# The gate of the layer's last stage as 2 by 2 block products with seven products

## The chip, the cores and the metric

One core of one Trainium2 chip runs the kernel; float32 data, batch 1, 512 tokens. The metric is the device time of one execution in microseconds (us). Before the change it is 706.38 us, the median of three runs (705.05 to 706.64).

## The reference, cut to what matters

One layer: three groups of attention heads with one input and one output projection, a gated MLP with a width-3 convolution, and a last stage that adds a gated per-layer embedding. The change is in the last stage, and in how the weights of the MLP's down projection are made ready.

```python
h = h + concat([o_a, o_b, o_c]) @ w_out[i]
h = h + conv_gated_mlp(rms_norm(h, ln_ffn[i]), w_up[i], conv_w[i], conv_b[i], w_down[i])
gate = sigmoid(rms_norm(h, ln_ple[i]) @ w_ple_gate[i])      # 512 x 1024 by 1024 x 1024
h = h + (p[i] @ w_ple_proj[i]) * gate
```

## The kernel before, in words

Activations lie transposed, features on the 128 partitions and the 512 tokens along the row. A float32 matrix product is made as three products of rounded parts (`mm3`): each operand is split into a high part, which ScalarE writes with a cast (rows `w_hi`, `Th`, `g_ah`, `xh`), and a low part, operand minus high part (rows `w_lo`, `Tl`, `g_al`, `xl`), and TensorE adds high by high, high by low and low by high. `split` (line 208) and `split_of` (line 1084) do this for weights: a load on SP's queue into one of 6 raw tiles, a cast on ScalarE, a subtraction on VectorE, and one of 7 pairs of high and low tiles that is free again when its last matmul has run.

**The stages.** Attention and the output projection, to about 290 us; a short stage that normalises; the up projection (tiles `u`), with the first parts of the down projection (tiles `dn_X`, `dn_Y`, `dn_Z`) among it, to 606 us; the rest of the down projection, to 653.9 us; the gate (tiles `pg`), to the end.

**Seven products.** The down projection works in 2 by 2 blocks: rows of weights in two halves (pairs of 128-row blocks), columns in two halves, tokens in two halves of `H` = 256. Seven products of block sums take the place of eight (`PRODUCTS`, `Down`, line 1338). The sums on the weights' side (`S1`, `S2`, `1e2e`, `1oS2`) are made in DRAM: copies on SP's queue during attention (`COPIES`, `copy_sum`), then 40 adding transfers on GpSimd's queue (`add_sums`, line 1185), one at a time: a semaphore holds each until the one before has landed. The sums on the activations' side are made by `left` (line 1206): four VectorE operations into tile `sm`, three casts and three low parts, 7 blocks of 256 columns for a pair of feature blocks. Each finished product is added to `h` by VectorE out of PSUM (`add_h`).

**The gate before.** `split3` casts and splits the finished `h` blocks into `Th` and `Tl`. `gate` takes 8 output blocks of 128 rows, 8 blocks of depth each, three matmuls of 512 columns; the last output block is done in two halves of 256. Weights come as 16 tiles of 512 columns (`row_weights`) with the gain `ln_ple` multiplied in while they are split. The norm's factor comes from squares of `h` (ScalarE), their sum (GpSimd, the last two on VectorE) and one matmul `pst`; it is multiplied onto each finished block, then the sigmoid, the product with the embedding (`ppl`, loaded on GpSimd's queue) and the addition of `h` follow.

**The order.** From the up projection on, every engine's order is made when the program is built: tasks with durations are placed by a planner (the loop at the end of the kernel) that knows engine times, ring slots and due times worked back from TensorE's order. It writes each engine's queue; on the chip each engine runs its queue in order.

Of the kernel before, what the change touches and what calls it, by code (L numbers as in the profile page):

```python
# [15 lines left out]
P = 128  # L16
# [50 lines left out]
_sums = sorted([(f, "u", f) for f in SEVEN] + [(PHASES[ph + 1] + 3, "d", ph) for ph in range(len(PHASES) - 1)])  # L67
# [11 lines left out]
def kernel(ctx: ExitStack, tc: tile.TileContext, x, xt0, xt, pt_in, small, bias_c,  # L79
                             w_in, w_out, w_up, w_usum, w_down, w_dsum, w_dadd, w_ple_gate, w_ple_proj, out):  # L80
# [68 lines left out]
    ROOM, NARROW = 128, 16  # L149
# [58 lines left out]
    def split(t, n, gain=None, to=None, eng=dve, c0=0, lead=None):  # L208

        if lead is not None:  # L210
            whole = [in_turn(q, NHI) for q in ("hi", "lo")]
            a, b = lead * P, (lead + 1) * P
            for i, j, c in ((0, a, c0), (a, b, 2 * c0), (b, n, 5 * c0)):
                if i < j:
                    hi, lo = (q[:, i + c : j + c] for q in whole)
                    act.copy(hi, t[:, i:j])
                    eng.tensor_tensor(out=lo, in0=t[:, i:j], in1=f32(hi), op=ALU.subtract)
            return whole
        hi, lo = to or [in_turn(q, NHI)[:, c0 : c0 + n] for q in ("hi", "lo")]
        if gain is None:  # L220
            act.copy(hi, t[:, :n])
            eng.tensor_tensor(out=lo, in0=t[:, :n], in1=f32(hi), op=ALU.subtract)
# [819 lines left out]
    COUNT = {"raw": NRAW, "hi": NHI, "conv": CONV, "pin": 1, "left": 3, "x": 3, "z": 2, "s": 2, "t": 3, "o": 1}  # L1042
# [17 lines left out]
    def tile_of(n, name, src=None, tag="raw", deps=()):  # L1060
# [4 lines left out]
        def do():  # L1065
            w.t = raw_tile() if tag == "raw" else mtmp(F32, 1, name)
            if src is not None:
                sp.dma_start(out=w.t[:, :n], in_=src)

        w.load = Task("load" if tag == "raw" else "side load", [("dma", n * 0.00139 if src is not None else 0)], do, deps, [w.raw])  # L1070
        return w

    class Group:


        def __init__(self, name):
            self.slot, self.tiles, self.name = Slot("left"), None, name

        def get(self, i, n):
            if self.tiles is None:  # L1080
                self.tiles = [q.rearrange("p j c -> p (j c)") for q in left_tiles(self.name)]
            return [q[:, i * S : i * S + n] for q in self.tiles]

    def split_of(w, deps=(), gain=None, group=None, i=0, c0=0):

        w.c0, w.lead = c0, None
        w.hi_slot = Slot("hi") if group is None else group.slot
        makes = [w.hi_slot] if not w.hi_slot.users else []

        def do():  # L1090
            w.hi, w.lo = split(w.t, w.n, gain, None if group is None else group.get(i, w.n), c0=c0, lead=w.lead)

        w.split = Task("do", [AC(w.n), DV(w.n * (1 if gain is None else 1.12))], do, (w.load, *deps), makes, [w.raw] + ([] if makes else [w.hi_slot]))
# [6 lines left out]
    def part(w, j, n=P):  # L1100
        c = j * n
        if w.lead is not None:
            c += w.c0 * (1 if j < w.lead else 2 if j == w.lead else 5)
# [28 lines left out]
    def down_weights(ph, n, name, tag="raw"):  # L1132
# [4 lines left out]
        return lambda what: split_of(tile_of(m, f"{name}_{what}", src[what], tag, SUM_TASKS.get(("d", ph), ()) if "S" in what or "2e" in what else ()), c0=NARROW)  # L1137

    def row_weights(src, name, gain=None, group=None, i=0):
        return split_of(tile_of(S, name, src), LAST_X if isinstance(group, Rest) else (), gain, group, i)  # L1140

# [43 lines left out]
    def add_sums(f):  # L1185
# [4 lines left out]
        def do(to, src):  # L1190
# [3 lines left out]
            if state:  # L1194
                tc.add_manual_dep(ins, state["last"].name, mybir.DependencyInfo(
                    mybir.DependencyClass.Sync, mybir.DependencyReason.DATA), reason="one adding transfer at a time")
            state["last"] = ins

        last = b
        for _, *key in _sums:  # L1200
            key = tuple(key)
            for to, src in add_parts(key):
                last = Task("add", [("pool", 1.2), ("acc", 3.2 if key[0] == "u" else 4.2)], lambda to=to, src=src: do(to, src), [last], (), [slot] if last is b else ())
                SUM_TASKS.setdefault(key, []).append(last)

    def left(f):

        tt = dve.tensor_tensor
        v = {}

        place, sums = Slot("left" if f < 18 else "x"), Slot("pin")

        def one():
            v["r"] = r1, r2 = G[f], G[f + 1]
            if f < 18:
                v["hl"] = left_tiles(f"g{f}")
            else:
                v["hl"] = tuple(q.rearrange("p a b c -> p (a b) c")[:, (f - 18) // 2 * 7 :][:, :7] for q in (Xh, Xl))
            hi, lo = v["hl"]
            v["sm"] = sm = mp.tile([P, 4, H], F32, tag="pin", bufs=1, name=f"sm_{f}")  # L1220
            tt(out=sm[:, 0], in0=r1[:, H:], in1=r1[:, :H], op=ALU.subtract)
            tt(out=sm[:, 2], in0=r2[:, :H], in1=r1[:, :H], op=ALU.subtract)
            act.copy(hi[:, 0], r1[:, H:])
            act.copy(hi[:, 1:3], r2.rearrange("p (j c) -> p j c", j=2))

        def two():
# [3 lines left out]
            act.copy(hi[:, 3:], sm)  # L1230
# [10 lines left out]

        (d1, s1), (d2, s2) = done_f[f], done_f[f + 1]
        a = Task("do", [DV(H), DV(H), AC(H), AC(S)], one, (d1, d2, LAST_X[0] if f >= 18 else None), [place, sums], [s1, s2])
        a = Task("do", [DV(H), DV(H), AC(2 * S)], two, [a], (), [s1, s2, place, sums])
        b = Task("do", [DV(H), DV(S)], three, [a], (), [s1, s2, place])
        c = Task("do", [DV(2 * S)], four, [a], (), [place, sums])
        CHAIN[f] = (b, c), place

# [296 lines left out]
    SPLIT3 = {}  # L1545

    def split3(n, b, c):

        g, ks, ts = n, slice(2 * c, 2 * c + 2), slice(b * H, (b + 1) * H)
        dh, dl = (T[g][:, ks, ts] for T in (Th, Tl))  # L1550

        def do():
            act.copy(dh, hblk(b, n, c))
            dve.tensor_tensor(out=dl, in0=hblk(b, n, c), in1=f32(dh), op=ALU.subtract)

        SPLIT3[n, b, c] = Task("do", [AC(S), DV(S)], do, [H_ADDS[n, q] for q, p in PRODUCTS.items() if p[3:5] == (b, c)] + ALL_UP)

    ALL_UP = [q for q in TASKS if q.kind == "pe"][-1:]
    sq_slots, sum_slot = [], Slot("pin")
    v3 = {}  # L1560

    def square3(j):

        s = Slot("conv")
        sq_slots.append(s)
        first = j == 0

        def do():
            if first:
                pin = mp.tile([P, D + 88], F32, tag="pin", bufs=1, name="sums3")  # L1570
                v3["sums"], v3["rb"] = pin[:, :S], pin[:, S:D]
            v3[j] = v3["sums"] if first else mtmp(F32, 1, f"n3_sq{j}")
            act.activation(v3[j], hj(j), AF.Square)
# [3 lines left out]

        deps = [H_ADDS[j // 4, q] for q, p in PRODUCTS.items() if p[4] == j // 2 % 2]
        if first:
            v3["last"] = Task("do", [AC(S)], do, deps, [sum_slot])  # L1580
        else:
            a = Task("do", [AC(S)], do, deps, [s])
# [5 lines left out]
    for b in range(2):  # L1588
        for c in range(2):
            split3(0, b, c)  # L1590
# [5 lines left out]
    for c in range(2):  # L1596
        for b in range(2):
            split3(1, b, c)
    for j in range(KD):
        square3(j)  # L1600
    pst_slot, root_slots = Slot("t"), [Slot("conv"), Slot("conv")]

    def sums3():
        v3["pst"] = total("t", v3["sums"])

    def roots3():
        roots(v3["pst"], v3["rb"], mtmp(F32, 1, "mt"), mtmp(F32, 1, "rsq"))

    def gate(j, c0, c1, at_k={}):
# [193 lines left out]
```

## Time and profile before

| what | value |
|---|---|
| median of three runs | 706.38 us |
| the profiled execution, as timed | 706.92 us |
| its span in the profile | 705.1 us |
| TensorE busy | 688.7 us (98%) |
| VectorE, ScalarE, GpSimd busy | 547.9, 395.5, 223.1 us |
| granted clock, mean | 0.997 |
| moved by DMA | 116.5 MB |

Times in the profile are us from the span's start. PE is TensorE, DVE VectorE, ACT ScalarE, POOL GpSimd, SPq the queue of SyncE that issues transfers. L105 is the line of a helper through which nearly all operations go, so rows are told apart by the names of tiles. A row of the timeline gives the start, the duration, and in brackets the idle time before it with what ended it. Durations of neighbouring rows overlap: an operation's issue is read from the difference of two starts.

### The profile page before, as it was taken

How to read it: one execution, taken by the hardware profiler on the slowest of the kernel's cores; microseconds unless marked ns; L12 is line 12 of the kernel's file. 1: busy time of each engine (PE TensorE's matmuls, PEld its weight loads, DVE VectorE, ACT ScalarE, POOL GpSimd, SP SyncE). 2: the span in 40 equal slices, each digit the busy share in tenths (PEclk: the TensorE clock that was granted, in tenths of full speed). 3: DMA queues.
4: the chain of work that ended last, by engine and by line, in shares of the span. 5: the costliest groups of instructions: out<-in, count | busy, mean ns of one | idle time of the engine just before them, and what ended most of it. 6: DMA issues, size and time to landing. Idle time of an engine off the chain costs nothing.

```text
span 705.1 us, 11575 instructions
## 1 busy us (share of the span) xinstructions
PE 688.7 (98%) x4028; PEld 616.2 (87%) x4028; DVE 547.9 (78%) x1123; ACT 395.5 (56%) x750; POOL 223.1 (32%) x324
## 2 busy tenths in 40 slices
PE   9999999999999999999999999999999999999997
PEld 8988888988999988868888899988988888999786
DVE  7668887888878875788878875798786787889764
ACT  6646766766656753565545653465444554646731
POOL 4676676767665440420110110110101110001310
PEclk9999999999999999999999999999999999999999
DMA  9453668746335213353686788787997675652531
GB/s 329 179 150 94 197 183 240 201 170 189 102 134 192 95 69 120 124 167 127 180 175 126 209 217 186 178 190 186 251 208 153 138 205 108 210 188 91 170 108 71
DMA packets 48471, 116.52 MB, mean 165 GB/s; under 512 B 5494, under 2 KB 7158, under 8 KB 48412
## 3 DMA queue, kind: packets, MB, share of 16 engines
q1 hardware_dynamic: 40476, 96.59, 42.3%
q0 software_dynamic: 7648, 18.88, 16.8%
q8 instruction: 32, 0.52, 0.3%
q10 hardware_dynamic: 288, 0.30, 0.1%
q14 instruction: 27, 0.22, 0.1%
HBM read 108.53 MB, written 31.47 MB: 199 GB/s over the span
## 4 chain that ended last, share of the span: by engine, by line
PE 78%; DVE 7%; DMA 6%; ACT 4%; POOL 2%; issue 2%; SPq 0%; DVEq 0%; ACTq 0%; POOLq 0%
PE u L105 30%; PE dn_X L105 8%; PE C_z L105 6%; PE pg L105 6%; PE wo L105 5%; PE dn_Y L105 4%; PE B_z L105 4%; PE dn_Z L105 2%; DMA bias_B<-fk_d 1%; DMA h<-in_x_dram 1%; PE sX L105 1%; PE A_z L105 1%; DMA waq<-in_w_in_dram 1%; PE C_s L105 1%; PE C_po L105 1%
## 5 line engine op out<-in xcount | busy, mean ns | idle before, releaser
L105 PE MATMUL u<-Tl,w_hi 128*128 128x512 f32 x320 | 125.0, 390 | 0.5 <-DVE Tl L105 0.5
L105 PE MATMUL u<-Th,w_hi 128*128 128x512 f32 x320 | 124.8, 390 | 0.0
L105 PE MATMUL u<-Th,w_lo 128*128 128x512 f32 x320 | 124.7, 390 | 0.0
L105 ACT CAST w_hi<-w_raw 128x768 fp32r<-128x768 f32 (+4 forms) x129 | 90.0, 724 | 58.0 <-PE u L105 17.7
L105 DVE TENSOR_TENSOR w_lo<-w_raw,w_hi 128x768 fp32r<-128x768 f32 (+3 forms) x127 | 102.7, 832 | 15.3 <-ACT w_hi L105 14.6
L105 DVE SCALAR_TENSOR_TENSOR c<-u,cols,c 128x511 f32<-128x511 f32 x80 | 59.7, 747 | 23.3 <-ACT c L105 22.3
L105 PEld LDWEIGHTS u<-Tl,w_hi 128*128 128x128 f32 x320 | 60.1, 188 | 13.4 <-DVE Tl L105 1.3
L105 PEld LDWEIGHTS u<-Th,w_lo 128*128 128x128 f32 x320 | 60.1, 188 | 12.6 <-POOL w_lo L105 0.2
L105 PEld LDWEIGHTS u<-Th,w_hi 128*128 128x128 f32 x320 | 60.1, 188 | 12.6 <-ACT Th L105 0.5
L105 ACT ACTIVATE c<-u,cols 128x512 f32<-128x512 f32 x40 | 31.1, 777 | 26.3 <-PE u L105 26.1
L105 POOL DMA_DIRECT2D dsum<-in_w_dadd_dram x16 | 13.1, 821 | 90.2 <-DMA dsum<-in_w_dadd_dram 64.8
L105 POOL DMA_DIRECT2D dsum<-dsum x16 | 13.0, 811 | 87.3 <-DMA dsum<-dsum 58.0
L105 PE MATMUL dn_X<-g_ah,w_hi 128*128 128x256 f32 x144 | 39.8, 277 | 0.0
L105 PE MATMUL dn_X<-g_ah,w_lo 128*128 128x256 f32 x144 | 39.8, 277 | 0.0
L105 PE MATMUL dn_X<-g_al,w_hi 128*128 128x256 f32 x144 | 39.8, 276 | 0.0
L105 PE MATMUL B_z<-B_h,Th 128*128 128x384 f32 x96 | 34.4, 358 | 0.8 <-DVE B_zn L105 0.6
L105 PE MATMUL C_z<-C_h,Th 128*128 128x384 f32 x96 | 34.2, 357 | 0.0
L105 PE MATMUL B_z<-B_h,Tl 128*128 128x384 f32 x96 | 32.4, 337 | 0.0
L105 PE MATMUL C_z<-C_h,Tl 128*128 128x384 f32 x96 | 32.3, 337 | 0.0
L105 PE MATMUL C_z<-C_l,Th 128*128 128x384 f32 x96 | 32.2, 336 | 0.0
L105 PE MATMUL B_z<-B_l,Th 128*128 128x384 f32 x96 | 32.2, 336 | 0.0
L105 PEld LDWEIGHTS dn_X<-g_al,w_hi 128*128 128x128 f32 x144 | 27.1, 188 | 0.3
(506 smaller groups left out, 2076.9 us busy)
## 6 DMA issues: line engine op xcount, KB each, us to landing
w_raw<-in_w_up_dram SPq DMA_DIRECT2D x44, 384.0 KB, 4.9
dsum<-in_w_dsum_dram SPq DMA_DIRECT2D x12, 768.0 KB, 6.8
w_raw<-dsum SPq DMA_DIRECT2D x24, 384.0 KB, 4.0
w_raw<-in_w_down_dram SPq DMA_DIRECT2D x18, 384.0 KB, 4.8
w_raw<-in_w_up_dram SPq DMA_DIRECT2D x20, 256.0 KB, 4.9
B_r<-in_w_in_dram SPq DMA_DIRECT2D x12, 384.0 KB, 3.7
C_r<-in_w_in_dram SPq DMA_DIRECT2D x12, 384.0 KB, 4.4
dsum<-in_w_dadd_dram POOLq DMA_DIRECT2D x12, 384.0 KB, 6.7
```

What stands on the lines that cost most here:

```text
L105: ins = getattr(self.eng, op)(*a, **k)
```

## The change

The gate is computed like the down projection. `h` times the gain goes through `left_blocks` (the body of `left`, now shared) for four pairs of feature blocks (`gate_left`): pairs 0 and 1 into the tiles `Th`/`Tl`, pairs 2 and 3 into the `g_ah`/`g_al` ring. Seven products for each of two halves of the output take three matmuls of 256 columns per pair and half; accumulators lie in the tags of `TAGS`. Weights come as tiles of 768 columns for pairs 0 to 2 and of three times 256 for pair 3, from `w_down4` (the gate's weights in the blocks' layout) or from sums in DRAM: 4 more copies (1 MB each) in the attention stage, and 8 more adding transfers of 512 KB. Adding transfers now wait for the one before the last, so two are under way. The products start with pairs 0 and 1 of the three that need no other result, in both halves; then pair 2, the norm's matmul, and pair 3.

Work that moves to GpSimd: the low parts of all 14 weight tiles of the down projection's last phase (`dn_...`, 512 columns), of 9 of the gate's 19 weight tiles (`BY_POOL`), four of the eight squares, and the two closing operations of three output blocks. GpSimd no longer issues the loads of `ppl`; SP does. In the planner, a task without VectorE work is now placed first if it can start before the next VectorE task.

The core of the diff:

```diff
-_sums = sorted([(f, "u", f) for f in SEVEN] + [(PHASES[ph + 1] + 3, "d", ph) for ph in range(len(PHASES) - 1)])
+_sums = sorted([(f, "u", f) for f in SEVEN] + [(PHASES[ph + 1] + 3, "d", ph) for ph in range(len(PHASES) - 1)]) + [(NF, "d", len(PHASES) - 1)]
+GATE = len(PHASES) - 1
...
-        return lambda what: split_of(tile_of(m, f"{name}_{what}", src[what], tag, SUM_TASKS.get(("d", ph), ()) if "S" in what or "2e" in what else ()), c0=NARROW)
+        return lambda what: split_of(tile_of(m, f"{name}_{what}", src[what], tag, SUM_TASKS.get(("d", ph), ()) if "S" in what or "2e" in what else ()), NARROW, pool if ph == 3 else None)
...
             ins = pool.dma_start(out=to, in_=src, accum_op=ALU.add, max_dma_last_dim=6144).ins
-            if state:
-                tc.add_manual_dep(ins, state["last"].name, mybir.DependencyInfo(
+            state["all"] = [*state.get("all", ()), ins]
+            if len(state["all"]) > 2:
+                tc.add_manual_dep(ins, state["all"][-3].name, mybir.DependencyInfo(
...
+            if j < 4:
+                pool.tensor_tensor(out=v3[j], in0=hj(j), in1=hj(j), op=ALU.mult)
+            else:
+                act.activation(v3[j], hj(j), AF.Square)
...
+    def gate_left(p):
+                act.activation(v[i], hj(2 * p + i), AF.Copy, scale=col(C_PLE, 2 * p + i))
...
+        left_blocks(("h", p), lambda: (v[0], v[1]), in_t if p < 2 else lambda: left_tiles(f"h{p}"), Slot("T" if p < 2 else "left"),
+                    hs + (ALL_UP if p < 2 else []), used, True)
...
+    def gate_product(n, what, pairs, w, b0, halves=(0, 1), begin=False, stop=False):
...
+            for i, p in enumerate(pairs):
+                hi, lo = LEFT["h", p]
+                for t in halves:
+                    q = accs[n, an][t % len(tags)]
+                    mm3(q[:, t * H : (t + 1) * H], *part(w, b0 + 2 * i + t), hi[:, li], lo[:, li],
+                        begin and i == 0 and t < len(tags), stop and i == len(pairs) - 1, skip_group_check=True)
...
+        e = pool if (n, what) in ((1, "1o"), (0, "1oS2"), (1, "1e2e")) else dve
...
+                e.tensor_tensor(out=y, in0=y, in1=pp, op=ALU.mult)
+                e.tensor_tensor(out=y, in0=y, in1=hblk(b, n, c)[:, t0:t1], op=ALU.add)
...
+    BY_POOL = {2, 4, 6, 8, 10, 12, 14, 16, 18}
...
+            main = [x for x, q in tr if any(e == "dve" for e, _ in q.parts)]
+            first_at = max(min(main, default=1e9), clock["dve"])
+            side = [(x, q) for x, q in tr if x < first_at and all(e != "dve" for e, _ in q.parts)]
+            if side:
+                tr, first_at = side, min(x for x, _ in side)
```

Three places show what the change makes of the engines' queues. First GpSimd's queue behind the last adding transfers, before the change (`sums` and `n_sq` belong to the norm; `ppl` are loads of the embedding):

```order
L105 DMA dsum_3484<-in_w_dadd_dram 128x512 x4
L105 DMA dsum_3484<-dsum_3484 128x512 x4
L105 TENSOR_TENSOR sums_7101<-sums_7101,n_sq_7103 128x512
L105 TENSOR_TENSOR sums_7101<-sums_7101,n_sq_7116 128x512
L105 TENSOR_TENSOR sums_7101<-sums_7101,n_sq_7184 128x512
L105 TENSOR_TENSOR sums_7101<-sums_7101,n_sq_7187 128x512
L105 TENSOR_TENSOR sums_7101<-sums_7101,n_sq_7189 128x512
L105 DMA ppl_0_7234<-pp_d 128x512
```

With the change ten low parts of `dn_...` tiles (weights of the down projection's last phase) stand directly behind the last adding transfer; then follow these rows, up to the first low part of a gate weight (`w_raw` of 128x768; `sums<-h` and `n_sq<-h` are squares):

```order
L106 TENSOR_TENSOR sums_4097<-h 128x512
L106 TENSOR_TENSOR n_sq_6977<-h 128x512
L106 TENSOR_TENSOR w_lo_3983<-dn_1_1o,w_hi_3982 128x512
L106 TENSOR_TENSOR sums_4097<-sums_4097,n_sq_6977 128x512
L106 TENSOR_TENSOR w_lo_4044<-dn_1_1e2e,w_hi_4043 128x512
L106 TENSOR_TENSOR n_sq_7064<-h 128x512
L106 TENSOR_TENSOR w_lo_3935<-dn_1_1oS_6777,w_hi_3934 128x512
L106 TENSOR_TENSOR n_sq_7135<-h 128x512
L106 TENSOR_TENSOR w_lo_3967<-dn_1_2o,w_hi_3966 128x512
L106 TENSOR_TENSOR sums_4097<-sums_4097,n_sq_7064 128x512
L106 TENSOR_TENSOR sums_4097<-sums_4097,n_sq_7135 128x512
L106 TENSOR_TENSOR w_lo_3990<-w_raw_3867,w_hi_3989 128x768
```

Where five additions and the issue of nine loads stood, 38 operations with two inputs in SBUF stand now (30 of 512 columns, 8 of 768), all of them behind the last adding transfer.

Second, VectorE in the down projection's last stretch, where the first half's sums into `h` end, before the change (`h<-h,dn_...` is an addition out of PSUM):

```order
L105 TENSOR_TENSOR h<-h,dn_0_X 128x2x256
L105 TENSOR_TENSOR w_lo_3914<-dn_1_S_6736,w_hi_3913 128x512
L105 TENSOR_TENSOR w_lo_3930<-w_raw_3862,w_hi_3929 128x768
L105 TENSOR_TENSOR w_lo_3946<-dn_1_S_6738,w_hi_3945 128x512
L105 TENSOR_TENSOR h<-h,dn_0_Y 128x2x256
L105 TENSOR_TENSOR w_lo_3962<-w_raw_3864,w_hi_3961 128x768
```

With the change (`sm_('h', 0)` are the block sums of pair 0, `hg` is `h` times the gain):

```order
L106 TENSOR_TENSOR h<-h,dn_0_X 128x2x256
L106 TENSOR_TENSOR w_lo_3935<-w_raw_3867,w_hi_3934 128x768
L106 TENSOR_TENSOR h<-h,dn_0_Y 128x2x256
L106 TENSOR_TENSOR sm_('h', 0)_6974<-hg_6969 128x256
L106 TENSOR_TENSOR sm_('h', 0)_6974<-hg_6972,hg_6969 128x256
L106 TENSOR_TENSOR w_lo_3967<-w_raw_3869,w_hi_3966 128x768
L106 SCALAR_TENSOR_TENSOR sm_('h', 0)_6974<-sm_('h', 0)_6974,hg_6972 128x256 x2
L106 TENSOR_TENSOR h<-h,dn_1_X 128x2x256
```

The low parts of 512 columns are gone from VectorE, and the sums of pair 0 stand between the additions into `h`.

Third, VectorE shortly before the gate begins, before the change:

```order
L105 TENSOR_TENSOR Tl_67<-h,Th_65 128x2x256
L105 SCALAR_TENSOR_TENSOR w_lo_3914<-w_raw_3866,cols,w_hi_3913 128x512
L105 TENSOR_TENSOR h<-h,dn_1_Y 128x2x256
L105 SCALAR_TENSOR_TENSOR w_lo_3930<-w_raw_3856,cols,w_hi_3929 128x512
L105 TENSOR_TENSOR Tl_67<-h,Th_65 128x2x256
L105 TENSOR_TENSOR h<-h,dn_1_X 128x2x256
```

With the change:

```order
L106 TENSOR_TENSOR Tl_66<-hg_6969,Th_64 128x256
L106 TENSOR_TENSOR Tl_66<-hg_6972,Th_64 128x512
L106 TENSOR_TENSOR Tl_67<-hg_7058,Th_65 128x256
L106 TENSOR_TENSOR Tl_67<-hg_7061,Th_65 128x512
L106 TENSOR_TENSOR Tl_67<-sm_('h', 1)_7139,Th_65 128x1024
L106 TENSOR_TENSOR h<-h,dn_1_X 128x2x256
L106 TENSOR_TENSOR w_lo_3983<-w_raw_3865,w_hi_3982 128x768
L106 TENSOR_TENSOR w_lo_4044<-w_raw_3869,w_hi_4043 128x768
L106 TENSOR_TENSOR h<-h,dn_1_Z 128x2x256
L106 TENSOR_TENSOR h<-h,dn_1_Y 128x2x256
```

Three additions into `h` of the second half, each of which a product of the down projection or of the gate waits for, now stand behind the low parts of pairs 0 and 1.

More of the change, by code (lines that the diff above doesn't have):

```diff
@@ L221, in split @@
             act.copy(hi, t[:, :n])
-            eng.tensor_tensor(out=lo, in0=t[:, :n], in1=f32(hi), op=ALU.subtract)
+            low = lambda: eng.tensor_tensor(out=lo, in0=t[:, :n], in1=f32(hi), op=ALU.subtract)
+            low() if lows is None else lows.append(low)
         else:
```

358 lines of the change are left out of this document (235 added, 123 removed).

## The prediction

> **What bounds the kernel now.** I read the page first, then busy time by stage, the chain that ended last, and the timelines around the end.
>
> ```profile
> PE 688.7 (98%) x4028; PEld 616.2 (87%) x4028; DVE 547.9 (78%) x1123; ACT 395.5 (56%) x750; POOL 223.1 (32%) x324
> 0.00:290.00 290.00, 280.77 (x1675) 259.01 (x1676) 221.72 (x638) 182.47 (x423) 166.68 (x262) 0.99 0.53 165
> 317.30:606.40 289.10, 289.10 (x1609) 252.34 (x1610) 228.81 (x350) 146.39 (x222) 33.12 (x41) 1.00 0.74 177
> 606.40:653.30 46.90, 46.90 (x416) 46.90 (x415) 41.10 (x61) 27.57 (x44) 2.80 (x2) 1.00 0.50 164
> 659.60:700.40 40.80, 40.72 (x199) 34.16 (x199) 25.54 (x40) 14.37 (x20) 3.30 (x6) 1.00 0.37 122
> ```
>
> The stage rows give length, then busy time of PE, PEld, DVE, ACT, POOL, the granted clock, and DMA share. TensorE has no hole from 317 us on, at full clock. Beside it VectorE stands at 41.1 of 46.9 us in the last of the down projection: nearly full. GpSimd is almost idle there, at 2.8 us.
>
> ```profile
> 598.75 0.39 PE L105 MATMUL u<-Th,w_hi 128*128 128x512 f32 x1
> 598.98 0.39 PE L105 MATMUL u<-Tl,w_hi 128*128 128x512 f32 x1
> 650.02 0.28 PE L105 MATMUL dn_Y<-xh,w_lo 128*128 128x256 f32 x1
> 650.13 0.28 PE L105 MATMUL dn_Y<-xh,w_hi 128*128 128x256 f32 x1
> 653.87 0.40 PE L105 MATMUL pg<-Th,w_hi 128*128 128x512 f32 x1
> 663.76 0.86 PE pst L105 x2
> 700.37 0.42 DVE L105 TENSOR_TENSOR y<-pg,sums 128x256 f32<-128x256 f32 x1 [1.08 <-PE pg L105]
> 701.74 0.42 DVE L105 TENSOR_TENSOR y<-y,h 128x256 f32<-128x256 f32 x1
> ```
>
> Durations mislead here (0.28 against 0.39): by the starts, a matmul of 512 columns takes a step of 0.227 us and one of 256 columns 0.1133 us, exactly half. So the smaller tiles of seven products cost TensorE nothing extra.
>
> **TensorE's part of the change.** The gate now has 168 matmuls of 512 and 48 of 256 columns: 168 x 0.227 + 48 x 0.1133 = 43.5 us. It will have 7 products x 2 halves x 4 pairs x 2 x 3 = 336 of 256: 38.1 us. It now runs from 653.87 to 700.37, 46.5 us, of which 0.86 is the norm's matmul and 2.1 waiting. Without any wait the new gate would end at 653.87 + 38.1 + 0.9 = 692.8; with the tail as now (700.37 to 705.1, 4.7 us) the span would be 697.5. That is the gain on offer, 7.6 us.
>
> **What pays for it: VectorE and GpSimd take turns.** Three pairs of rows show what a GpSimd operation does to VectorE.
>
> ```profile
> 306.51 1.84 POOL L105 TENSOR_TENSOR w_lo<-w_raw,w_hi 128x768 fp32r<-128x768 f32 x1 [7.34 <-ACT w_hi L105]
> 306.56 2.34 DVE L105 SCALAR_TENSOR_TENSOR rb_ah<-rb_al,rb_ah 128x512 f32<-128x512 f32 x1
> 642.90 1.30 POOL L105 TENSOR_TENSOR sums<-sums,n_sq 128x512 f32<-128x512 f32 x1 [52.65 <-ACT n_sq L105]
> 643.35 1.40 DVE L105 TENSOR_TENSOR w_lo<-dn_2o,w_hi 128x512 fp32r<-128x512 f32 x1
> 294.30 1.45 POOL L105 TENSOR_TENSOR sums<-sums,sq 128x512 f32<-128x512 f32 x1 [0.26 <-ACT sq L105]
> 294.51 0.67 DVE L105 TENSOR_TENSOR h<-h,wo 128x512 f32<-128x512 f32 x1
> 295.11 1.19 DVE L105 TENSOR_TENSOR w_lo<-w_raw,w_hi 128x512 fp32r<-128x512 f32 x1
> ```
>
> VectorE's operations with both inputs in SBUF, 0.69 us undisturbed, come out 1.65, 0.72 and 0.51 us late, and each ends about 0.55 us after the GpSimd operation that it met: it waits until that one is over. The addition at 294.51, whose second input (`wo`) lies in PSUM, is not held up. So a GpSimd operation takes the turn for about 1.17 us at 512 columns (642.90 to 643.35 + 0.72) and 1.70 at 768 (306.51 to 306.56 + 1.65).
>
> [...]
>
> VectorE's own prices:
>
> ```profile
> 610.52 0.42 DVE L105 TENSOR_TENSOR sm<-c 128x256 f32<-128x256 f32 x1
> 610.85 0.42 DVE L105 TENSOR_TENSOR sm<-c,c 128x256 f32<-128x256 f32 x1
> 611.19 0.88 DVE L105 SCALAR_TENSOR_TENSOR sm<-sm,c 128x256 f32<-128x256 f32 x2
> 613.18 1.22 DVE L105 TENSOR_TENSOR xl<-sm,xh 128x1024 fp32r<-128x1024 f32 x1 [1.12 <-ACT xh L105]
> 614.33 0.68 DVE L105 TENSOR_TENSOR w_lo<-dn_1e,w_hi 128x512 fp32r<-128x512 f32 x1
> 624.60 0.95 DVE L105 TENSOR_TENSOR w_lo<-w_raw,w_hi 128x768 fp32r<-128x768 f32 x1
> 625.47 0.69 DVE L105 TENSOR_TENSOR w_lo<-dn_2o,w_hi 128x512 fp32r<-128x512 f32 x1
> 626.07 0.68 DVE L105 TENSOR_TENSOR w_lo<-dn_1e,w_hi 128x512 fp32r<-128x512 f32 x1
> ```
>
> By the starts: 0.34 for 256 columns, 0.60 for 512, 0.87 for 768, 1.15 for 1024; block sums and low parts of one pair (0.34 + 0.34 + 0.74, then 1.15 + 0.34 + 0.60) 3.5 us.
>
> **The turns from 610.5 us on** (the block sums of the up projection's last pair; the first GpSimd low part can't begin before, since `dn_1e` is issued at 604.48 and such loads take 5.0 us).
>
> ```profile
> 604.48 0.42 SPq L105 DMA_DIRECT2D dn_1e<-in_w_down_dram  x1
> dn_1e<-in_w_down_dram SPq DMA_DIRECT2D x2, 256.0 KB, 5.0
> ```
>
> GpSimd, after the change: 14 low parts of the down projection, 4 squares, 5 additions to the norm's sum, one gate low part and 6 closing operations at 512 columns, 30 x 1.17 = 35.1; 8 gate low parts at 768, 13.6. Together 48.7. VectorE: 9 low parts of the down projection and 10 of the gate at 768, 16.5; five pairs (the up projection's last and the gate's four) at 3.5, 17.5; 2 sums, 3 steps of the norm's root, 6 multiplications with the norm and 10 closing operations at 0.60, 12.6. Together 46.6. Sum 95.3 us. For the gate and the low parts this is not a relief: a 512-column low part takes 0.60 us of the turn on VectorE and 1.17 on GpSimd.
>
> Back to back, the last turn ends at 610.5 + 95.3 = 705.8; the output's transfer follows (2.9 us, from 701.74 + 0.42 to 705.1): span 708.7, if no turn is ever idle. Since TensorE would be through at 692.8, **the turn becomes the bound**.
>
> How much of it stays idle I worked out by laying the rows end to end in the order of the queues, each when its engine, its input and the turn are free. Three lows of `dn` tiles get between the sums of the last up pair and its low parts: 610.5 + 1.4 + 0.95 (the cast on ScalarE) + 2.1 + 3 x 1.17 + hand-overs = 618.6, where TensorE needs them at 616.6: 2.0 late. From there to the low parts of pair 1, 35.9 us of turns are due (11 low parts, 7 squares and sums, 9 low parts, two pairs); they end at 659, and the additions into `h` that stand behind them on VectorE hold up the down projection's last products: the gate starts at about 663, 9.1 late. Then TensorE waits 3.1 for pair 2's low parts and 2.4 for a weight's, and 4.5 in the last products. The sum, 19 us, puts TensorE's end near 712, and VectorE's remaining operations near 716.7. So 10.9 us of the 106 are idle; I take 9, as the rows overlap a little more than I counted (0.95 long, the next one 0.87 later). Span: 705.8 + 9 + 2.9 = 717.7.
>
> **The other parts.** ScalarE has more casts but is at 27.6 of 46.9 us; cost nothing, and if that cover went, the weights' casts (0.75 each) would come late singly. Loads of `ppl` on SP wait behind outputs only; they are needed two operations later; nothing to 1 us. The 4 MB of copies more in attention stand between loads on SP's queue; DMA is 0.53 busy there: nothing, bound 2 us. The planner's rule moves the rows shown and else little.
>
> The adding transfers stand ahead of all of GpSimd's low parts:
>
> ```profile
> 336.22 0.95 POOL L105 DMA_DIRECT2D dsum<-in_w_dadd_dram  x1
> 589.44 0.81 POOL L105 DMA_DIRECT2D dsum<-dsum  x1 [3.82 <-DMA dsum<-dsum]
> dsum<-in_w_dadd_dram POOLq DMA_DIRECT2D x12, 384.0 KB, 6.7
> q0 software_dynamic: 7648, 18.88, 16.8%
> ```
>
> 40 in 253 us are 6.3 each, nearly the 6.7 that one takes to land. 48 (the last 8 a third larger, so some 50.7 of the old size) must be through by about 610: 5.4 each. With two under way the step is 3.2 if landing stays as it is, 6.3 if it doubles. The engines' time allows 16.8% of 705 us for 18.88 MB, 2.5 us for 384 KB, and they are 0.74 busy now. I take 4: the last lands near 540. Cost nothing.
>
> [...]
>
> **The rivals.** *TensorE stays the bound* (faster): the turns don't collide, because VectorE's additions out of PSUM and its waits lie beside GpSimd's work and the 38 operations find gaps. Then 697.5 of span, 699.3 as timed. For it: VectorE alone, freed of 14 low parts, fits. Against: the sum of 95.3 in the 87 us between 610.5 and 697.5. It decides only if a GpSimd operation holds the turn for less than about 0.9 us instead of 1.17. *The turns pack tightly*: no idle and a VectorE turn shorter by 0.06: 75 of them save 4.5, span 704.2, no change. *The adding transfers don't go faster at two* (slower still): step 6.3, the last at 336 + 50.7 x 6.3 = 655, the first low part 40 us late: 745. Against: 0.26 of the engines' time is free.
>
> **How the numbers follow.** The forecast, a span of 717.7, is 719.5 as timed (706.92 against 705.1 of span), and 719.0 against the median, which lies 0.5 below the profiled execution. Chances: the turn bounds with idle time 0.78, tight 0.05, TensorE bounds 0.14, transfers 0.03. The upper bound of the likeliest: all 24 operations of VectorE out of PSUM (0.6 each) find no GpSimd work beside them, 708.7 + 14.4, plus 2 for the copies: 725.1 of span, 726.4. The range, 704 to 727, leaves out TensorE's case and the transfers'. Within 0.2% is about what a measurement of this kernel can tell from no change: faster 0.15, same 0.05, slower 0.80.
>
> **What would show it.** Right: in the timeline from 610 us on, GpSimd busy for more than 50 us, VectorE's operations of 512 columns at 1.2 us and more beside it, TensorE waiting for `Tl`, `h_al`, `w_lo` and for `h` before the gate and in it. TensorE's steps of 0.1133 in the gate, 336 of them. Adding transfers through by 560. Wrong: VectorE at 0.69 us beside GpSimd's low parts, a gate without holes, or an end below 704.

## The result, and the profile after

| | before | after |
|---|---|---|
| time as timed, median (range), us | 706.51 (705.05 to 707.66) | 724.44 (722.19 to 724.51) |
| ratio, with its 95% interval | 1 | 1.0247 (1.022 to 1.0275) |
| span of the profiled execution (as timed), us | 705.1 (706.92) | 722.7 (724.51) |
| mean granted clock of TensorE | 0.997 | 0.986 |

The change costs 2.5%, some 18 us. The forecast was 719.0, in a range of 704 to 727.

The first line of the page after, and busy time by stage: the down projection's last phase, the gate, and what follows TensorE's last matmul. The stages are cut at TensorE's own marks, for the kernel before first and then for the kernel after; the columns are length, then busy time of PE, PEld, DVE, ACT and POOL, granted clock, DMA share and GB/s.

```profile
606.40:653.80 47.40, 47.40 (x421) 47.40 (x420) 41.29 (x61) 28.07 (x45) 3.17 (x3) 1.00 0.50 164
653.80:700.20 46.40, 45.16 (x221) 37.62 (x219) 30.82 (x44) 19.81 (x30) 8.80 (x12) 1.00 0.37 121
700.20:705.10 4.90, 0.13 (x2) 0.00 (x0) 1.28 (x3) 0.42 (x1) 0.00 (x0) 0.96 0.15 52
```

```profile
PE 689.8 (95%) x4148; PEld 622.5 (86%) x4148; DVE 573.5 (79%) x1125; ACT 406.7 (56%) x769; POOL 282.4 (39%) x356
605.40:663.70 58.30, 51.29 (x421) 50.75 (x421) 49.56 (x51) 28.18 (x43) 37.41 (x23) 0.94 0.44 139
663.70:714.10 50.40, 43.60 (x341) 41.88 (x339) 44.65 (x52) 30.04 (x47) 24.17 (x14) 0.93 0.49 154
714.10:722.70 8.60, 0.13 (x2) 0.00 (x0) 4.76 (x9) 1.38 (x3) 1.86 (x2) 0.63 0.36 122
```

All of the loss lies behind the up projection, which ends 1.0 us earlier than before. The down projection takes 58.3 us instead of 47.4, the gate 50.4 instead of 46.4, though it has 5.4 us less of matmuls, and the tail 8.6 instead of 4.9: -1.0 + 10.9 + 4.0 + 3.7 = 17.6, the difference of the spans. In the first stage GpSimd went from 3.2 to 37.4 us, and VectorE is busy longer although it lost 14 operations.

The timelines of VectorE and of GpSimd at the start of the down projection show the turns (columns: start, us, engine, line, operation; in brackets the idle time ahead of it):

```profile
609.73 1.52 DVE L106 TENSOR_TENSOR sm<-c 128x256 f32<-128x256 f32 x1
611.17 1.51 DVE L106 TENSOR_TENSOR sm<-c,c 128x256 f32<-128x256 f32 x1
...
615.74 2.13 DVE L106 TENSOR_TENSOR xl<-c,xh 128x256 fp32r<-128x256 f32 x2
617.79 2.04 DVE L106 TENSOR_TENSOR w_lo<-w_raw,w_hi 128x768 fp32r<-128x768 f32 x1
619.75 0.68 DVE L106 TENSOR_TENSOR h<-h,dn_X 128x512 f32<-128x512 f32 x1
```

```profile
609.42 1.55 POOL L106 TENSOR_TENSOR w_lo<-dn_1e,w_hi 128x512 fp32r<-128x512 f32 x1 [78.55 <-ACT w_hi L106]
610.94 1.46 POOL L106 TENSOR_TENSOR w_lo<-dn_S,w_hi 128x512 fp32r<-128x512 f32 x1
615.89 1.42 POOL L106 TENSOR_TENSOR w_lo<-dn_S,w_hi 128x512 fp32r<-128x512 f32 x1 [3.49 <-ACT w_hi L106]
617.28 1.73 POOL L106 TENSOR_TENSOR w_lo<-dn_1o,w_hi 128x512 fp32r<-128x512 f32 x1
```

A block sum of 256 columns takes 1.5 us where it took 0.42; a low part of 768 columns 2.04 where it took 0.95; the addition out of PSUM keeps its 0.68. GpSimd pays too (1.4 to 1.7 beside VectorE, 1.28 with VectorE idle, at 628.53). The pauses of TensorE that come of it, from its timeline:

```profile
620.57 0.36 PE L106 MATMUL dn_X<-g_ah,w_hi 128*128 128x256 f32 x1 [2.00 <-DVE h L106]
...
658.96 0.55 PE L106 MATMUL dn_X<-g_ah,w_hi 128*128 128x256 f32 x1 [3.37 <-DVE h L106]
...
681.96 0.39 PE L106 MATMUL g_X<-h_ah,w_lo 128*128 128x256 f32 x1 [3.65 <-DVE w_lo L106]
...
684.33 0.58 PE L106 MATMUL g_X<-h_ah,w_lo 128*128 128x256 f32 x1 [1.60 <-DVE w_lo L106]
684.70 0.42 PE L106 MATMUL g_Y<-h_ah,w_hi 128*128 128x256 f32 x1
684.92 0.41 PE L106 MATMUL g_Y<-h_al,w_hi 128*128 128x256 f32 x1
...
713.95 0.28 PE L106 MATMUL g_X<-h_ah,w_lo 128*128 128x256 f32 x1
```

TensorE waits for `h` in the down projection (7.0 us) and in the gate for weights' low parts (5.2), for `gk`, the gate's sums on their way to the output (1.1), and for `h_al` (0.5): 13.8 us that the trace names. The starts behind the fourth of these pauses are 0.21 us apart, not 0.113. Two of the windows of 2 us there say why (granted clock is the third number from the end):

```profile
684.00:686.00 2.00, 1.67 (x8) 1.68 (x9) 2.00 (x4) 0.60 (x1) 0.00 (x0) 0.50 0.34 52
686.00:688.00 2.00, 2.00 (x11) 2.00 (x11) 1.93 (x5) 0.60 (x1) 0.00 (x0) 0.50 0.95 320
```

Behind these pauses TensorE runs at half its clock (0.50 in both rows). The three stretches of it (620.8 to 624.3, 659.3 to 661.9, 684.3 to 689.1) last 10.9 us and cost 0.47 of that (1 - 0.113/0.213), 5.1 us. In the profile of before the granted clock is 0.50 from 45.9 to 49.3 us, in attention, and nowhere from there to the end of the gate; the forecast has no term for it.

The adding transfers, first and last issue on GpSimd, and how long they take to land:

```profile
342.60 1.80 POOL L106 DMA_DIRECT2D dsum<-in_w_dadd_dram  x2
...
530.06 0.81 POOL L106 DMA_DIRECT2D dsum<-dsum  x1 [2.67 <-DMA dsum<-dsum]
```

```profile
dsum<-in_w_dadd_dram POOLq DMA_DIRECT2D x12, 384.0 KB, 8.0
```

48 issues, 47 steps in 187.5 us, are 4.0 a step, though each lands later than before (8.0 against 6.7). They end long ahead of the low parts.

### The profile page after: what moved, and what is told of

Same layout as the page of the kernel before. It is cut to its first block, busy times and chain, and to the rows that moved or that the text cites. A ratio compares the mean times of both kernels' runs of the same rounds, so it can differ in the third digit from the quotient of the medians.

```text
span 722.7 us, 11923 instructions
## 1 busy us (share of the span) xinstructions
PE 689.8 (95%) x4148; PEld 622.5 (86%) x4148; DVE 573.5 (79%) x1125; ACT 406.7 (56%) x769; POOL 282.4 (39%) x356
## 4 chain that ended last, share of the span: by engine, by line
PE 74%; DVE 15%; ACT 4%; issue 3%; POOL 2%; DMA 2%; DVEq 0%; POOLq 0%; ACTq 0%
PE u L106 29%; PE C_z L106 6%; PE dn_X L106 6%; PE wo L106 6%; PE B_z L106 4%; PE A_z L106 3%; PE dn_Y L106 3%; DVE w_lo L106 3%; PE g_X L106 2%; PE dn_Z L106 1%; PE g_Y L106 1%; PE sX L106 1%; PE B_s L106 1%; PE C_s L106 1%; PE B_po L106 1%
## 5 line engine op out<-in xcount | busy, mean ns | idle before, releaser
L106 DVE TENSOR_TENSOR w_lo<-w_raw,w_hi 128x768 fp32r<-128x768 f32 (+4 forms) x138 | 125.1, 928 | 18.9 <-ACT w_hi L106 17.9
L106 ACT CAST w_hi<-w_raw 128x768 fp32r<-128x768 f32 (+4 forms) x149 | 104.0, 731 | 56.2 <-PE dn_X L106 13.3
L106 PE MATMUL dn_X<-g_ah,w_hi 128*128 128x256 f32 x144 | 41.5, 288 | 7.0 <-DVE h L106 7.0
L106 POOL DMA_DIRECT2D dsum<-dsum x20 | 16.3, 814 | 65.1 <-DMA dsum<-in_w_dadd_dram 33.0
L106 POOL DMA_DIRECT2D dsum<-in_w_dadd_dram x20 | 17.1, 868 | 56.4 <-DMA dsum<-in_w_dadd_dram 36.7
L106 POOL TENSOR_TENSOR w_lo<-w_raw,w_hi 128x768 fp32r<-128x768 f32 (+1 forms) x11 | 22.3, 2037 | 35.7 <-ACT w_hi L106 32.1
L106 PEld LDWEIGHTS dn_X<-g_ah,w_hi 128*128 128x128 f32 x144 | 28.4, 197 | 7.7 <-issue 4.0
L106 POOL TENSOR_TENSOR w_lo<-dn_1e,w_hi 128x512 fp32r<-128x512 f32 x2 | 2.8, 1414 | 78.5 <-ACT w_hi L106 78.5
```

The lines of the kernel that those rows point to most:

```text
L106: ins = getattr(self.eng, op)(*a, **k)
```

## The experiments

| kernel | what it is | median, us | ratio to before (95%) |
|---|---|---|---|
| after | the change | 724.44 | 1.022 to 1.0275 |
| e1 | all of GpSimd's new work back to VectorE and ScalarE | 717.02 | 1.0132 to 1.0169 |
| e2 | only the down projection's low parts back | 716.74 | 1.0118 to 1.0167 |
| e3 | only the gate's low parts back | 722.14 | 1.020 to 1.024 |
| e4 | only squares and closing operations back | 724.03 | 1.0222 to 1.0287 |
| e5 | e1 without low parts of the gate's weights | 701.99 | 0.9925 to 0.9959 |
| e6 | e1, gate's low parts due 4 us earlier | 714.08 | 1.0087 to 1.0132 |
| e7 | before, with the down projection's low parts on GpSimd | 707.81 | 1.0014 to 1.0049 |
| e8 | after, adding transfers one at a time | 754.21 | 1.0626 to 1.0724 |
| e9 | e1, 8 of the gate's low parts by transfer | 715.65 | 1.0127 to 1.0163 |
| e10 | e1, 16 of them by transfer | 720.22 | 1.0192 to 1.0223 |
| e11 | after, GpSimd's low parts read one input | 708.28 | 1.0019 to 1.0051 |
| e12 | e9 with three due times changed | 713.76 | 1.0103 to 1.0141 |

Each ratio is against executions of the kernel before that were timed beside that run, with medians of 705.15 to 706.59 us; so a difference of two medians across the table can be off by up to 1.4 us.

Where the time goes, from the starts of the gate's first and of TensorE's last matmul in each profiled execution:

| | first gate matmul | gate, first to last | last matmul to the end |
|---|---|---|---|
| before | 653.9 | 46.2 | 5.0 |
| after | 663.8 | 50.2 | 8.7 |
| e1 | 653.3 | 55.7 | 5.7 |
| e2 | 655.4 | 50.1 | 8.8 |
| e3 | 664.4 | 49.3 | 5.4 |
| e4 | 658.8 | 61.0 | 5.1 |
| e5 | 652.8 | 38.8 | 7.6 |
| e6 | 654.9 | 49.0 | 8.0 |
| e9 | 651.8 | 56.0 | 5.0 |
| e10 | 654.1 | 54.8 | 10.6 |
| e11 | 655.6 | 42.5 | 8.7 |
| e12 | 654.5 | 48.0 | 8.6 |

### e1: GpSimd's new work back where it was

```diff
-NARROW, pool if ph == 3 else None)
+NARROW, None)
-BY_POOL = {2, 4, 6, 8, 10, 12, 14, 16, 18}
+BY_POOL = set()
-if j < 4:
-    pool.tensor_tensor(out=v3[j], in0=hj(j), in1=hj(j), op=ALU.mult)
-else:
-    act.activation(v3[j], hj(j), AF.Square)
+act.activation(v3[j], hj(j), AF.Square)
-e = pool if (n, what) in ((1, "1o"), (0, "1oS2"), (1, "1e2e")) else dve
+e = dve
```

> The seven-product gate stays; the 14 low parts of the down projection, the 9 of the gate and the 6 closing operations go back from GpSimd to VectorE, the 4 squares to ScalarE. Theory of turns: from 610.5 us on GpSimd keeps 5 additions x 1.17 = 5.9 us of turns, VectorE has 46.6 + 14 x 0.60 + 0.60 + 8 x 0.87 + 6 x 0.60 = 66.2; together 72, which end at 682.5, before TensorE's 692.8. So TensorE is the bound again: a span of 697.5 to 701.5 (waits of up to 4 us between planned tasks), 699 to 703 us as timed, below the kernel before. Rival A (the block-product gate itself is what costs: its sums, low parts and closing operations make a longer chain than the plain gate): the time stays at 718 or more. Rival B (the stalls come from the changed order of issue, not from the engine that does the work): 712 to 720.

Measured: 717.02, only 7.4 us better than after and 10.4 us worse than before; that is in rival B's range and 1 us short of rival A's. Its down projection is whole again (48.3 us), its gate is worse than in after. The stages of e1:

```profile
604.90:653.20 48.30, 48.01 (x420) 47.84 (x420) 41.47 (x63) 29.28 (x46) 4.01 (x3) 1.00 0.50 157
653.20:709.10 55.90, 45.11 (x341) 43.66 (x339) 48.49 (x71) 31.28 (x50) 2.67 (x2) 0.91 0.51 156
709.10:714.70 5.60, 0.14 (x2) 0.00 (x0) 2.43 (x7) 0.75 (x2) 0.00 (x0) 0.76 0.28 94
```

VectorE is busy for 48.5 us in a gate for which TensorE needs 39. And what it does first is not what TensorE waits for: ScalarE's last cast of a weight, two closing operations on VectorE, the low part behind them, and the matmul that waited for it, from the timelines of the three engines in e1:

```profile
687.25 0.81 ACT L106 CAST w_hi<-w_raw 128x768 fp32r<-128x768 f32 x1
...
699.31 0.69 DVE L106 TENSOR_TENSOR gk<-gk,ppl 128x512 f32<-128x512 f32 x1 [0.69 <-ACT gk L106]
...
700.65 0.68 DVE L106 TENSOR_TENSOR gk<-gk,sums 128x512 f32<-128x512 f32 x1
701.25 0.95 DVE L106 TENSOR_TENSOR w_lo<-w_raw,w_hi 128x768 fp32r<-128x768 f32 x1
702.26 0.58 PE L106 MATMUL g_X<-Th,w_lo 128*128 128x256 f32 x1 [4.59 <-DVE w_lo L106]
```

Every cast was over by 688.1, this low part came at 701.25, behind closing operations that themselves wait for TensorE and ScalarE. So taking GpSimd's work away mends the down projection, and not the gate: with all of it on VectorE, that engine's queue alone makes TensorE late. A sum of turns that comes to less than TensorE's time does not mean that TensorE is the bound. What the turns cost in the gate while GpSimd keeps its share, e1 can't say; e11 does.

### e2, e3, e4: one part of it back at a time

e2 is the first line of e1's diff, e3 the second, e4 the rest.

> Only the 14 low parts of the down projection's last phase go back to VectorE; the gate's 9 low parts, the squares and the closing operations stay on GpSimd. Theory of turns: 14 x (1.17 - 0.60) = 8 us of turns less, all of it ahead of the gate: the three waits for h in the down projection (7.0 us) and the half clock behind them shrink, the gate starts at 655 to 657 instead of 663.8, and the end comes 6 to 9 us earlier: 715 to 718 us. The gate's own waits for w_lo (5.2 us) remain. Rival A (the gate itself): no change, 723 to 725, with the gate earlier but its end where it was.

> Only the gate's 9 low parts go back to VectorE; those of the down projection stay on GpSimd. Theory of turns: 14.8 us of GpSimd's turns go and 7.6 of VectorE's come, 7 us less, most of it behind 663 us. The down projection's waits for h stay (7.0 us, gate start 661 to 664), the 5.2 us for w_lo and the half clock behind them go; gate 39 us and tail 4.7: span 706 to 709, 708 to 711 us as timed. Rival A (the gate itself): 722 to 725.

> Only the 4 squares go back to ScalarE and the 6 closing operations to VectorE. Theory of turns: 10 x 1.17 = 11.7 us of GpSimd's turns go, 3.6 of VectorE's come: 8.1 us less, of which the squares' 4.7 lie in the stretch 642 to 656 ahead of the gate; 716 to 720 us. Rival A: 722 to 725.

Measured: e2 716.74, 7.7 us better, as the turns say (8.0), and all of it ahead of the gate, which starts at 655.4. e3 722.14: the gate's start stays, and of the 14 us that I expected behind it 2.3 came. e4 724.03: no change that could be told from none; TensorE's waits for `w_lo` grow to 14.2 us in the gate (in a profiled execution of 727.55, 3.5 us above the median). Both lie in the range of rival A, the gate itself. In the gate, moving work between the two engines trades one wait for another: TensorE ends at 705.6 in e2, 709.1 in e1, 713.9 in e3, 714.1 in after and 719.9 in e4.

### e5: is it VectorE's work or the loads?

```diff
-mm3(q[...], *part(w, b0 + 2 * i + t), hi[:, li], lo[:, li],
+wh = part(w, b0 + 2 * i + t)[0]
+mm3(q[...], wh, wh, hi[:, li], lo[:, li],
-w.split = Task("do", [low], lambda: [q() for q in w.lows], [a], (), [w.hi_slot, w.raw])
+w.split = a
```

> The kernel of e1_all_dve without the low parts of the gate's weights: they are not computed, and the gate's products read the high part in their place (same number of matmuls, another result). VectorE loses 18 operations of 768 columns and 3 of 512 or less, about 17 us behind 640 us; casts, loads and their buffers stay. Theory V (VectorE's queue, which the low parts of the gate's larger weights fill, is what holds up the gate): the waits for w_lo in the gate (2.4 + 3.7 + 4.6 us) and the half clock behind them (5 us) go: 717.0 - 10.7 - 5 = 701, 699 to 704. Rival L (the loads of 14 instead of 8 half megabytes through 6 buffers, with casts on ScalarE, are what is late): TensorE waits for w_hi instead, 709 or more.

Measured: 701.99, theory V, and 4.0 us faster than the kernel before beside it. The stage of the gate in e5:

```profile
652.70:691.80 39.10, 39.10 (x341) 38.53 (x339) 31.38 (x49) 30.02 (x50) 3.41 (x2) 1.00 0.67 213
```

With the same loads, casts and buffers TensorE has no hole, and the gate takes 39.1 us: within a tenth of the forecast's 38.1 + 0.9. 16.4 us of VectorE's operations less (91.3 to 74.9 us from 606 us to the end) are 15.0 us of time less. This is no version to use, since the low parts are part of the result.

### e6: the same work in another order

```diff
+w.split.sooner = 4.0
...
+x += getattr(q, "sooner", 0.0)
```

> The kernel of e1_all_dve with one number of the planner changed: a gate weight's low part is due 4 us earlier, so that VectorE issues it ahead of closing operations that wait for TensorE or ScalarE. Theory V1 (VectorE has the time, only the order in its queue is wrong): the waits of 3.7 and 4.6 us for w_lo and the half clock behind them shrink, nothing takes their place: 704 to 710. Theory V2 (VectorE has too much work there): others come late instead (h, h_al, the norm's root, the closing operations), 713 to 720.

Measured: 714.08, at V2's end. The waits for `w_lo` fell to 2.1 us, and others came in their place. TensorE's waits in e6 from 650 us on:

```profile
PE g_X L106 <- DVE w_lo L106: 2.1, 1, 2.1
PE g_X L106 <- DVE h_al L106: 1.5, 2, 1.3
PE g_X L106 <- DVE h L106: 1.1, 1, 1.1
PE g_Y L106 <- DVE h_al L106: 0.8, 1, 0.8
```

TensorE's end came 5 us earlier (703.9), but the closing operations that were put back now lengthen the tail from 5.7 to 8.0 us.

### e7: the turns in the kernel before

```diff
-w.split = Task("do", [AC(w.n), DV(w.n * (1 if gain is None else 1.12))], do,
+low = DV(w.n * (1 if gain is None else 1.12)) if eng is None else ("pool", 0.1 + w.n * 0.0026)
+w.split = Task("do", [AC(w.n), low], do,
...
-c0=NARROW)
+c0=NARROW, eng=pool if ph == 3 else None)
```

> The kernel before with one part of the change: the 14 low parts of the down projection's last phase go from VectorE to GpSimd. Theory of turns: 14 x (1.17 - 0.60) = 8.0 us more of turns in a stretch of 46.9 us in which VectorE was busy for 41.1; less the 5.8 us that were free, 2 us at least, and up to 8 where additions into h get behind; 709 to 715. Rival (GpSimd's work lies beside VectorE's, and relieves it): 705 to 707.

Measured: 707.81, 1.8 us slower than the 705.97 of the kernel before beside it, 0.14% to 0.49%. The sign is that of the turns, the size below my range. The same 14 operations cost 7.7 us in the kernel after (e2 against after). The difference is probably what else VectorE has to do there, since in after the block sums and low parts of the pairs stand in the same stretch; no run tries this by itself.

### e8: one adding transfer at a time

```diff
-if len(state["all"]) > 2:
-    tc.add_manual_dep(ins, state["all"][-3].name, ...
+if len(state["all"]) > 1:
+    tc.add_manual_dep(ins, state["all"][-2].name, ...
```

> The kernel after, with the adding transfers one at a time as before (the order of all else unchanged). Theory of the prediction: the step goes from 3.9 to about 6.3 us, 48 transfers from 342.6 us end near 650, and GpSimd's low parts, which stand behind them in its queue, begin some 40 us late: 745 to 770. Rival (one at a time lands faster, in 4 us, so the step stays): 722 to 727.

Measured: 754.21. The last transfer's issue and the first low part behind it on GpSimd, and how a transfer lands, in e8:

```profile
645.70 0.81 POOL L106 DMA_DIRECT2D dsum<-dsum  x1 [5.54 <-DMA dsum<-dsum]
646.25 1.55 POOL L106 TENSOR_TENSOR w_lo<-dn_1e,w_hi 128x512 fp32r<-128x512 f32 x1
```

```profile
dsum<-in_w_dadd_dram POOLq DMA_DIRECT2D x12, 384.0 KB, 6.5
```

From 343.71 to 645.70 are 302 us, 6.4 for each of 47 steps; TensorE waits 30.6 us for that low part. Two at a time is what the rest of the change stands on.

### e9, e10: low parts by another way

```diff
+act.copy(w.hi, w.t[:, : w.n])
+act.activation(w.lo, w.t[:, : w.n], AF.Copy, scale=-1.0)
+pool.dma_start(out=w.lo, in_=w.t[:, : w.n], accum_op=ALU.add)
```

In both kernels the planner is also told that these low parts are due 3 us earlier.

> The kernel of e1_all_dve, with 8 of the gate's 19 weight tiles given their low part by neither VectorE nor a GpSimd operation: ScalarE writes minus the high part (one operation more of 0.73 us each), and an adding transfer from GpSimd's queue adds the weight, as the attention does for some of its weights (such transfers landed in 7.1 us). VectorE loses 8 x 0.87 = 7.0 us in the gate. Theory V (VectorE's queue holds up the gate; e5, which lost all low parts, came to 702): about half of e5's gain, 717.0 - 7 to 9 = 708 to 710. Rival (a buffer is held some 7 us longer, so that loads come late): 714 or more.

> As e9, with 16 of the 19 tiles. VectorE loses about 13.5 us in the gate. Theory V: near e5's 702, 701 to 706, faster than the kernel before by up to 0.7%. Rival: each tile holds its buffer for about 6 (load) + 1.5 (two operations of ScalarE) + 7 (transfer) = 14.5 us, 6 buffers give a tile each 2.4 us against the 2.05 us that TensorE takes for one: 16 x 0.35 = 5.6 us late and a half clock behind it, 708 to 716, and TensorE's waits name the transfers.

Measured: 715.65 and 720.22. Both miss theory V's numbers; e9 lies in its rival's range, though no wait of TensorE names a load, and e10 lies above its rival's too. VectorE was relieved (from 606 us to the end its busy time falls from 91.3 us in e1 to 84.4 and 78.6), and the transfers land in 5.6 and 6.0 us; but TensorE now waits elsewhere. Its waits in e10 from 650 us on:

```profile
PE g_X L106 <- ACT gk L106: 4.1, 1, 4.1
PE g_Y L106 <- ACT gk L106: 1.9, 1, 1.9
PE g_X L106 <- DMA w_lo<-w_raw: 1.5, 1, 1.5
```

`gk` is ScalarE's copy of an accumulator, which must be out before the next product adds to it; it now stands behind more casts. In e9 the waits are for `h_al` (4.2 us) and again for a low part behind closing operations (4.4).

### e11: the same GpSimd operations with one input

```diff
-eng.tensor_tensor(out=lo, in0=t[:, :n], in1=f32(hi), op=ALU.subtract)
+eng.tensor_scalar(lo, f32(hi), 0.0, 0.0, ALU.mult, ALU.mult) if eng is pool else ...
```

> The kernel after, in which GpSimd's operation for a low part reads one input only (the high part, times zero), so that these low parts are zero: GpSimd has an operation at the same place with the same dependencies, but no second SBUF input. If what holds VectorE up is that both engines read two inputs from SBUF: VectorE's operations beside these take 0.69 us (512) and 0.95 (768) again, and the time falls to about that of e1 and e2, 715 to 718. If any operation of GpSimd holds VectorE up: as long as it takes, with 0.8 us in place of 1.2 per 512 columns, 719 to 723.

Measured: 708.28, below both ranges and 16.2 us faster than after by the medians (15.0 by the two ratios), with every operation on the same engine and in the same order. The edit also reaches two low parts that GpSimd makes of the up projection's first weights, at 306 and 310 us; the up projection ends about 0.7 us earlier. GpSimd and VectorE side by side in e11, the same place as above, and GpSimd's operation by itself:

```profile
613.79 3.05 POOL L106 TENSOR_SCALAR w_lo<-w_hi 128x512 fp32r<-128x512 f32 x3 [3.15 <-ACT w_hi L106]
...
624.58 0.62 POOL L106 TENSOR_SCALAR w_lo<-w_hi 128x512 fp32r<-128x512 f32 x1 [0.68 <-ACT w_hi L106]
```

```profile
613.63 1.44 DVE L106 TENSOR_TENSOR xl<-c,xh 128x256 fp32r<-128x256 f32 x2
614.99 1.36 DVE L106 TENSOR_TENSOR w_lo<-w_raw,w_hi 128x768 fp32r<-128x768 f32 x1
```

VectorE is still held up, by 0.42 us (1.44 against 1.02) and 0.41 (1.36 against 0.95), where two inputs held it up by about 1.1 each. So it is not the second input alone that decides, as the first of the two theories had it; a turn is shorter with it gone. Whether it is the missing input or the shorter operation (0.62 us against 1.28) that does it, the run can't separate. VectorE's operations are the same as in after, and its busy time from 606 us to the end falls from 98.4 to 83.2 us: these 15.2 us are what the shorter turns save it, about as much as the time gained. By another count, 15 turns shorter by 0.75 and 8 by about 1.1 (1.70 to some 0.6, an estimate from GpSimd's 0.83 us for 768 columns) are 20 us. The low parts of GpSimd are zero here, so this is no version to use either.

### e12: half by transfer, and other due times

```diff
+b.sooner = c.sooner = 3.0
+w.split.sooner = 3.0
-outs[-1].early = 0.0 if (n, what) == (1, "2o") else 4.0
+outs[-1].early = 0.0
```

> The kernel of e9_half_by_transfer with three of the planner's numbers changed: the low parts of the gate's block sums and of its weights are due 3 us earlier, and the closing operations only at the end instead of 4 us ahead of it. So the low parts of pair 3 stand ahead of the norm's root, for whose matmul VectorE waited 2.6 us in e9, and the last weight's low part stands ahead of the closing operations, behind which it came 4.4 us late. Theory V1 (with half of the gate's low parts gone VectorE has the time, and what was left of the waits is order): the 8.6 us of waits in e9's gate and the 5 to 6 us of half clock go for the most part: 701 to 706, the same as the kernel before or 0.5% faster. Theory V2 (VectorE's work still doesn't fit): new waits in their place, 711 to 716.

Measured: 713.76, theory V2. TensorE's end comes 5.3 us earlier than in e9 (702.5 against 707.8), the tail grows by 3.6 us, and ScalarE's copy of an accumulator is a new wait of 2.9. No version that I found keeps the result and beats the kernel before; the nearest with seven products in the gate, e6 and e12, are 1.1% and 1.2% slower.

## Why the prediction was right, and where it was wrong

**TensorE's part** held: 336 matmuls at a step of 0.1133 us, and without waits a gate of 39 us, which e5 shows. Of the 7.6 us on offer e5 got 5.9 in the profiled executions (span 699.2 against 705.1; 4.0 by the medians), since its tail is 7.4 us instead of 4.9: of the last product VectorE closes a half and two quarters one behind the other.

**The turns** held in the down projection. The forecast put the gate's start at about 663, 9.1 us late; it was 663.8. That it came so near is in part luck: of the 10.9 us by which the stage grew the trace names 7.0 as waits, and 2.9 are half clock (0.47 of 6.1 us), for which the 9.1 had no term. e2 gives the start back to within 1.5 us, and e11 shows that it is how long GpSimd's operations hold VectorE up. What the forecast did not say is that the same turns have another price in another kernel: 7.7 us here, 1.8 in e7.

**The gate** is where the reasoning fell short, although its numbers nearly fit: TensorE's end was forecast near 712 and came at 714.1. The waits were laid out in other places: 3.1 us for pair 2's low parts, 2.4 for a weight's and 4.5 in the last products, where the trace has 0.5 for `h_al`, 5.2 for weights' low parts and 1.1 for `gk`. The step that failed is the one in the rival "TensorE stays the bound": "VectorE alone, freed of 14 low parts, fits". It does not: e1 has all turns but five gone and its gate takes 55.7 us. So the turns becoming the bound was right for after, but a sum of turns below TensorE's time (e1's 72 us) did not make TensorE the bound: I had counted turns, not VectorE's queue. The sum of 95.3 us left out the 24 operations out of PSUM (14.4 us), since GpSimd does not hold them up (one took 0.68 us beside it in after, at 619.75, and 0.69 without it in before, at 618.03); but the low parts stand behind them all the same. And a sum of busy times says nothing of order: low parts wait behind closing operations that wait for TensorE. e5 shows that VectorE's work on the gate's low parts is the cause in e1: take it away, and 15 us go. e11 shows the other half, that of after: with short turns on GpSimd, which carries 9 of the 19 tiles, the gate takes 42.5 us instead of 50.2. Both engines together nearly keep up there; with turns of 1.17 and 1.70 us they do not.

The same rival's condition, that it decides if GpSimd holds the turn for less than about 0.9 us, was tried by e11, whose low parts hold it for about 0.4 at 512 columns (squares, sums and closing operations stay as they were): 708.3, not the rival's 699.3.

**Two terms were missing**: the half clock behind TensorE's pauses, 5.1 us, and a tail of 8.6 instead of 5.7 us (712 to 717.7), because a closing operation of GpSimd and those of the half stand ahead of the last quarters on VectorE. The first was made up for by waits that I had laid out too long: 19 us in the forecast, 13.8 named by the trace, 5.1 of half clock, and 3.4 that no view names, in part what a pause takes beyond its wait (starts lie 4.03 us apart around a wait of 3.65). That these errors offset each other is luck. The second is most of the 5.0 us by which the span of 717.7 was too short.

**The adding transfers** held: a step of 4 forecast, 4.0 measured, the last issued at 530; the rival's 745 for one at a time is 754 in e8. **The copies in attention** cost nothing: the up projection ended 1.0 us earlier.

What stays open: why e9 and e10, which take 6.9 and 12.7 us of busy time from VectorE where e5 takes 16.4, give so little back or nothing. The waits name ScalarE's queue, and e12 that order is worth something (1.9 us from e9); no run had ScalarE's copies freed as well.

## What to carry to other kernels

An idle engine is no room if its operations hold the full one up, as GpSimd's did here (2.04 us for a low part of VectorE that took 0.95 without them): price the move by what the full engine loses per operation, in the stage where it lands (the same 14 operations cost 1.8 us in one kernel and 7.7 in the other). Fewer matmuls mean more operands to make: count every operation of the engine that makes them, those out of PSUM too, and look at what stands ahead of each operand in its queue, not only at busy time. And a pause of TensorE can be paid for again behind it, at half the clock: in after pauses of 2.0 to 3.7 us had 10.9 us of it behind them, which cost 5.1 us.

## What was not expected of the hardware

Behind three of TensorE's pauses in after its granted clock was 0.50, with steps of 0.213 us for 256 columns in place of 0.113. The changes lay on a grid of 3.41 us (620.83, 624.24, 658.38, 661.79, 682.27 and 689.10: all differences are multiples of that), and ahead of each of the three falls to 0.50 among them went a window of this grid in which TensorE had little to do (busy for 1.41, 0.62 and 0.31 of 3.41 us). Two neighbouring windows of after, and then two of e3, where a pause of the same length (2.27 us from start to start, against 2.28) had no such sequel; the third column is TensorE's busy time, and the third number from the end the granted clock:

```profile
617.42:620.83 3.41, 1.41 (x13) 1.24 (x12) 3.41 (x4) 1.52 (x3) 3.41 (x2) 1.00 0.53 144
620.83:624.24 3.41, 3.41 (x18) 3.41 (x18) 3.41 (x3) 0.00 (x0) 2.08 (x2) 0.50 0.96 319
```

```profile
619.59:623.00 3.41, 1.54 (x13) 1.57 (x14) 3.41 (x4) 0.46 (x1) 3.41 (x3) 1.00 0.63 165
623.00:626.40 3.40, 3.40 (x32) 3.40 (x31) 3.40 (x4) 1.46 (x2) 1.43 (x2) 1.00 0.89 314
```

In the traces of all these runs, from 600 us to TensorE's last matmul, each of the 23 windows at full clock in which TensorE was busy for less than 0.44 of the time was followed by one at 0.50; of the five between 0.45 and 0.52 one was (e9), and of the windows above 0.52 none. So the pause of 2.28 us in after had half the clock behind it, and that of 2.27 in e3, which lay elsewhere on the grid, had not.

In e11 a GpSimd operation with one SBUF input (0.62 us at 512 columns) held VectorE up for 0.4 us (1.44 against 1.02 us, 1.36 against 0.95); in after one with two (1.28 us) did so for about 1.1 (2.13 against 1.02, 2.04 against 0.95).

Two adding transfers under way at once landed in 8.0 us each against 6.5 one at a time (after, e8), and still went through at 4.0 us a piece against 6.4.
